# Down projection summed on VectorE in running PSUM sums, norm roots on GpSimd, and tails with a new order

## The chip, the cores and the metric

The kernel runs on one core of one Trainium2 chip. The metric is the device time of one execution, in microseconds (us). A core has TensorE (PE: matrix multiplications from SBUF into PSUM), VectorE (DVE) and ScalarE (ACT) for elementwise work, GpSimd (POOL), and SyncE (SP), which here issues the transfers between DRAM and SBUF. Each engine takes its instructions in order and waits for semaphores of the others.

## What is computed

A two-layer encoder on 1024 rows of width 1024, in float32. Each layer is a mixing half (dilated attention beside latent attention in layer 0, a gated block beside neighbourhood attention in layer 1) and a dense FFN of hidden width 2816. Every half starts with an RMSNorm.

```python
def _rmsnorm(x, g):
    y = xf * lax.rsqrt(jnp.mean(xf * xf, -1, keepdims=True) + EPS) * g
...
    for layer in range(DEPTH):
        h = _rmsnorm(x, norm_mix[layer])
        ...
            x = x + jnp.concatenate([a_out, b_out], -1) @ ev_w_out[j]
        ...
            x = x + jnp.concatenate([c_out, d_out], -1) @ od_w_out[j]
        h = _rmsnorm(x, norm_ffn[layer])
        gu = h @ ffn_w_gu[layer]
        x = x + (jax.nn.silu(gu[..., :FFN_HIDDEN]) * gu[..., FFN_HIDDEN:]) @ ffn_w_down[layer]
    return _rmsnorm(x, final_gain)
```

## The kernel before

Every float32 multiplication is made as three: an operand is split into a high part (ScalarE copies it, rounded, L61) and a low part (VectorE or GpSimd subtracts, L62), and `mm3` (L67 to L71) multiplies high by high, low by high and high by low into one PSUM tile. Large products use Winograd's scheme: both matrices are cut into quarters, seven products of sums of quarters are formed instead of eight, and sums of these give the result.

The **projections** (gate and up of the FFN, and those into a layer) are lists of `Block`s. A block makes the seven weight operands (`combo`), multiplies each with an activation operand and adds up (`post`). The activation operands are named after their sums: `B1` (a first quarter pair), `T0` to `T3` (four sums), `B2`; each has a high and a low part (`B1h`, `B1l`). Product 1 and 2 use `B1`, 5 `T0`, 6 `T1`, 7 `T2`, 4 `T3`, 3 `B2`. `FIRST` is the order of the seven in the first block.

A **tail** stands at the end of each half that feeds the next norm. `tail` goes over eight tiles of 128 rows in the order 0, 1, 4, 2, 5, 3, 6, 7. In each it multiplies the last four chunks of the contraction (24 matmuls of 128x512), adds into x (L1038), takes the norm (`norm_pre`: square with its sum on ScalarE, `rstd_from_ssq`, then `nh` on VectorE, L121), transposes the normed tile on TensorE two tiles later (`ops_tile`, L967) and makes the operands from the transposed tile: tiles 0 to 3 give `B1` and a raw copy `rw`, tiles 4 to 7 with the raw copy of the tile four before give `T0` to `T3` and `B2`. The last two tiles and the first projection products are interleaved by `first`. There are three such tails (tail 1 behind layer 0's output projection, tail 2 behind its FFN, tail 3 behind layer 1's output projection), and one that ends in the output instead of operands; its last tile is worked by halves (`last_tile`).

The **root** (`rstd_from_ssq`) is a square root on ScalarE, a reciprocal on VectorE and one Newton step in four more VectorE instructions.

The **down projection** (`down`) takes 18 of the FFN's 22 chunks of 128 in Winograd's scheme (the other four are the tail's). Seven products, each in five groups of two chunks (the last of one); an item is one product and group, two chunks by four row tiles by three, 24 matmuls. It reads hidden activations `a1`, `a2` and a streamed `st` (from the DRAM tile `hS`) and weights `b1`, `b2`, `b3`. `prep` makes the two operands and their splits, two items ahead of the matmuls; `load` issues the transfers four items ahead. The order of products is 1, 7, 5, 6, 2, 3, 4. A product's two PSUM tiles are added into the quarters of x that need it (`post`). GpSimd makes the sums of the activations (L1227, L1231, L1235, L1239) and six sums into x (L1273); VectorE makes those of the weights (L1228, L1232, L1236, L1242) and the splits.

The order on each engine is set by a scheduler from the order in which the program is written and its priorities; `high_priority` raises a part.

## Time and profile before

| | us |
|---|---|
| median of 3 runs (2534.26 to 2544.32) | 2538.3 |
| profiled execution | 2536.99 |
| its span | 2535.2 |
| TensorE busy | 2427.9 (96%) |
| VectorE busy | 1815.4 (72%) |
| ScalarE busy | 1095.0 (43%) |
| GpSimd busy | 422.5 (17%) |

The busy share is an average over stages. A stage is read from the table by stretches: its length, less the time in which TensorE is busy, is time in which TensorE stood still there. PEclk is the mean clock granted to TensorE, 1.00 being 2.4 GHz and 0.50 being 1.2 GHz. The view of waits then says which instruction waited, on which engine's instruction, and for how long.

### The profile page before, as it was taken

The numbers are of one execution on the slowest core, as the hardware profiler recorded it, in microseconds if no ns is written. First come the engines' busy times: TensorE is split into PE (matmuls) and PEld (weight loads), VectorE is DVE, ScalarE is ACT, GpSimd is POOL, SyncE is SP. The second block draws the span as 40 slices with busy tenths as digits, with TensorE's granted clock in tenths as the row PEclk, the third lists the DMA queues.
The fourth block names the chain that finished last, engine by engine and source line by source line (L and its number), as shares of the span: only waits on it lengthen the run. The fifth ranks groups of instructions, "written<-read, shape, count | busy, mean of one in ns | idle before, by whom it ended". The sixth has DMA issues, their size and how long they took to land.

```text
span 2535.2 us, 31630 instructions
## 1 busy us (share of the span) xinstructions
PE 2427.9 (96%) x12205; PEld 2047.1 (81%) x12205; DVE 1815.4 (72%) x2324; ACT 1095.0 (43%) x1691; POOL 422.5 (17%) x247
## 2 busy tenths in 40 slices
...
GB/s 259 154 195 222 270 172 142 109 141 72 116 185 92 65 99 100 50 100 222 205 54 142 120 164 162 127 180 202 197 107 100 64 87 100 62 140 271 75 63 67
DMA packets 199670, 345.76 MB, mean 136 GB/s; under 512 B 12936, under 2 KB 122728, under 8 KB 199264
## 3 DMA queue, kind: packets, MB, share of 16 engines
...
## 4 chain that ended last, share of the span: by engine, by line
PE 71%; DVE 15%; ACT 4%; issue 4%; DMA 4%; POOL 2%; SPq 0%; DVEq 0%; ACTq 0%; POOLq 0%
PE b L69 20%; PE b L70 20%; PE b L71 20%; DVE wl L62 3%; PE m L807 2%; PE b L693 2%; PE b L791 2%; DMA T2l<-rpk 1%; PE m L732 1%; PE b L711 1%; DVE bPl L62 1%; DVE T2h L62 1%; DVE xt L1038 1%; POOL rw L991 1%; DMA raw<-in_ffn_w_gu_dram 1%
## 5 line engine op out<-in xcount | busy, mean ns | idle before, releaser
L61 ACT ACTIVATE wh<-sr 128x1024 fp32r<-128x1024 f32 (+1 forms) x121 | 126.1, 1045 | 348.7 <-PE b L70 325.2
L1751 DVE TENSOR_TENSOR u<-u,b 128x1024 f32<-128x1024 f32 (+1 forms) x119 | 141.2, 1204 | 139.5 <-PE b L71 139.4
L61 ACT ACTIVATE wh<-raw 128x1024 fp32r<-128x1024 f32 (+1 forms) x102 | 105.9, 1050 | 244.2 <-PE b L70 135.3
L62 DVE TENSOR_TENSOR wl<-sr,wh 128x1024 fp32r<-128x1024 f32 (+1 forms) x121 | 146.0, 1209 | 53.1 <-ACT wh L61 52.9
L70 PE MATMUL b<-B1l,wh 128*128 128x512 f32 x440 | 171.7, 390 | 0.8 <-DVE rs_v L97 0.8
L69 PE MATMUL b<-B1h,wh 128*128 128x512 f32 x440 | 171.4, 390 | 0.0
L71 PE MATMUL b<-B1h,wl 128*128 128x512 f32 x440 | 171.3, 389 | 0.0
L1227 POOL TENSOR_TENSOR B2l<-raw,T3h 128x1024 f32<-128x1024 f32 x2 | 6.9, 3442 | 816.2 <-PE b L70 816.2
L70 PE MATMUL b<-wl,wh 128*128 128x512 f32 x336 | 132.1, 393 | 7.8 <-DVE wl L62 7.7
L71 PE MATMUL b<-wh,wl 128*128 128x512 f32 x336 | 130.9, 389 | 0.0
L69 PE MATMUL b<-wh,wh 128*128 128x512 f32 x336 | 130.8, 389 | 0.0
L69 PE MATMUL b<-wh,mh 128*128 128x512 f32 x320 | 128.7, 402 | 0.8 <-DVE B1l L1057 0.8
L62 DVE TENSOR_TENSOR wl<-raw,wh 128x1024 fp32r<-128x1024 f32 (+1 forms) x96 | 115.3, 1210 | 17.9 <-ACT wh L61 17.4
L70 PE MATMUL b<-wl,mh 128*128 128x512 f32 x320 | 127.5, 398 | 0.0
L71 PE MATMUL b<-wh,ml 128*128 128x512 f32 x320 | 127.1, 397 | 0.1
L70 PEld LDWEIGHTS b<-B1l,wh 128*128 128x128 f32 x440 | 82.6, 188 | 18.7 <-DVE B1l L973 1.7
L71 PEld LDWEIGHTS b<-B1h,wl 128*128 128x128 f32 x440 | 82.6, 188 | 17.0
L69 PEld LDWEIGHTS b<-B1h,wh 128*128 128x128 f32 x440 | 82.6, 188 | 17.0
L62 DVE TENSOR_TENSOR bPl<-b,bPh 128x1024 fp32r<-128x1024 f32 x64 | 78.0, 1220 | 13.0 <-ACT bPh L61 12.4
L70 PEld LDWEIGHTS b<-wl,wh 128*128 128x128 f32 x336 | 63.1, 188 | 25.4 <-DVE wl L62 12.6
L69 PE MATMUL b<-T1h,wh 128*128 128x512 f32 x192 | 75.6, 394 | 7.5 <-ACT wh L61 7.5
L784 DVE CUSTOM_DVE_ANT_0 bP<-b,zero 128x1024 f32<-128x1024 f32 x64 | 77.9, 1217 | 6.7 <-PE b L71 4.2
...
## 6 DMA issues: line engine op xcount, KB each, us to landing
raw<-in_ffn_w_gu_dram SPq DMA_DIRECT2D x88, 512.0 KB, 5.0
hS<-hid SPq DMA_DIRECT2D x44, 512.0 KB, 2.9
xt<-xp SPq DMA_DIRECT2D x24, 512.0 KB, 4.3
x<-xt SPq DMA_DIRECT2D x24, 512.0 KB, 2.7
raw<-in_od_w_in_dram SPq DMA_DIRECT2D x20, 512.0 KB, 6.1
raw<-kS SPq DMA_DIRECT2D x16, 512.0 KB, 6.7
st<-hS SPq DMA_DIRECT2D x16, 512.0 KB, 4.0
raw<-in_ev_w_in_dram SPq DMA_DIRECT2D x14, 512.0 KB, 5.0
```

The source lines that it names most:

```text
L61: nc.scalar.activation(hi, src, AF.Copy)
L62: (eng or nc.vector).tensor_tensor(lo, src, hi.bitcast(F32), ALU.subtract)
L69: mm(ps, lhsT=l[0], rhs=r[0], start=start, stop=False)
L70: mm(ps, lhsT=l[0], rhs=r[1], start=False, stop=False)
L71: mm(ps, lhsT=l[1], rhs=r[0], start=False, stop=stop)
L693: nc.tensor.matmul(sp[:, tt, j0:j1], lhsT=q, rhs=k[l], start=l == 0, stop=l == 1)
L711: nc.tensor.transpose(tp[:, pos], sb[:, tt, kc * P:(kc + 1) * P], self.ident)
L732: nc.tensor.matmul(o, lhsT=v, rhs=pt[l][:, pp], start=first, stop=last)
L784: nc.vector.tensor_tensor_reduce(pr, sp, self.zero.to_broadcast([P, S]), 1.0, 3e38, ALU.add, ALU.min, st[:, 0, hd, t:t + 1])
L791: nc.tensor.transpose(tp[:, kc], pr[:, kc * P:(kc + 1) * P], self.ident)
L807: nc.tensor.matmul(o, lhsT=V[:, kc], rhs=pt[l][:, kc], start=(kc == 0 and l == 0), stop=(kc == KC - 1 and l == 1))
L1751: add = lambda o, x: k.nc.vector.tensor_tensor(o, x, pb, ALU.add)
```

## The change

- **Root**: a scaling on GpSimd (VectorE where there are eight columns) and a power with exponent -0.5 on GpSimd take the place of ScalarE's root and VectorE's five steps.
- **Tail**: the last two tiles' `nh` are made on VectorE like the others (`VIAP` goes); the fourth tile's split of `B1` is made from PSUM at raised priority, ahead of the raw copy, and its transposes and those of the last two tiles no longer stand early; of the two sums into the raw copy of tiles 4 to 7 one (`x[0]`) moves from GpSimd to VectorE; the x buffer is three deep, and the operand sum of product 5 uses it. `FIRST` becomes 1, 2, 5, 4, 6, 7, 3, and the low parts of products 1 and 2 of the first block move from GpSimd to VectorE.
- **Down**: the order of products becomes 1, 5, 6, 3, 7, 2, 4. Products 1, 6, 7, 4 add up in the same PSUM tiles without a reset, and so do 5, 3. After each product its running sum is added into one quarter of x. All operand sums are on VectorE. `st` is streamed for products 5, 3, 7 and 4, and `b2` is loaded a second time into `B2h` for product 7.
- **Last tile**: each half has a PSUM tile of its own; x is multiplied by the gain before the root is known; then ScalarE scales one half and VectorE the other.

```diff
         r = self.t(pool, [P, w], F32, "rs_r")
-        nc.scalar.activation(s, ssq, AF.Sqrt, scale=1.0 / n, bias=self.eps)
-        nc.vector.tensor_scalar(v, ssq, 1.0 / n, EPS, ALU.mult, ALU.add)
-        nc.vector.reciprocal(r, s)
...
+        (nc.gpsimd if w == 1 else nc.vector).tensor_scalar(r, ssq, 1.0 / n, EPS, ALU.mult, ALU.add)
+        nc.gpsimd.tensor_tensor(r, r, self.mhalf[:, :w], ALU.pow)
         return r
...
         if t < 4:
+            with self.tc.high_priority(offset=200) if t == 3 else nullcontext():
+                self.split(o["B1"][0][:, :, sl], o["B1"][1][:, :, sl], pt)
             raw = raws[t] = self.t(wk, [P, 8, P], F32, "rw", bufs=self.rwb)
             nc.scalar.activation(raw, pt, AF.Copy)
-            nc.scalar.activation(o["B1"][0][:, :, sl], pt, AF.Copy)
-            tt_(o["B1"][1][:, :, sl], raw, o["B1"][0][:, :, sl].bitcast(F32), ALU.subtract)
             return
...
         T = [self.t(wk, [P, 4, P], F32, "tt", bufs=2) for i in range(2)]
-        tt_(T[0], pt[:, :4], raw[:, :4], ALU.subtract)
+        x = [raw[:, 4 * i:4 * i + 4] for i in range(2)]
+        tt_(T[0], pt[:, :4], x[0], ALU.subtract)
         tt_(T[1], pt[:, 4:], T[0], ALU.subtract)
-        for i in range(2):
-            x = raw[:, 4 * i:4 * i + 4]
-            nc.gpsimd.tensor_tensor(x, T[1], x, ALU.subtract)
...
+        nc.gpsimd.tensor_tensor(x[1], T[1], x[1], ALU.subtract)
+        tt_(x[0], T[1], x[0], ALU.subtract)
+        for i, y, eng in ((0, T[0], None), (3, x[1], nc.gpsimd), (1, T[1], None), (2, x[0], None), ("B2", pt[:, 4:], None)):
+            self.split(o[i][0][:, :, sl], o[i][1][:, :, sl], y, eng=eng)
...
-            elif p[0] in HPS:
-                with self.tc.high_priority(offset=HPO):
-                    self.ops_tile(wk, ps, p[1], p[0], raws)
             else:
...
             if out is None:
-                x = self.t(wk, [P, D], F32, "xt", bufs=2)
+                x = self.t(wk, [P, D], F32, "xt", bufs=3)
                 self.dma(nc.sync, x, xpart[sl])
...
                 self.split(m[0][:, ks], m[1][:, ks], msrc[:, ks, sl], eng=nc.gpsimd)
+            if out is not None and n == 7:
+                self.last_tile(wk, m, ws, [self.t(ps, [P, 2, 512], F32, "b")[:, 0] for i in range(2)], x, gain, out[sl])
+                break
             pb = self.t(ps, [P, 2, 512], F32, "b")
-            if out is not None and n == 7:
-                self.last_tile(wk, m, ws, pb, x, gain, out[sl])
-                break
             for k in range(4):
...
                 self.dma(nc.sync, xdst[sl], x)
-            hist.append((t, self.norm_pre(wk, x, gain, pb.rearrange("p c n -> p (c n)") if n in VIAP else None)))
+            hist.append((t, self.norm_pre(wk, x, gain)))
             if out is not None:
...
             for k in range(4):
-                self.mm3(pb[:, cc], (m[0][:, k], m[1][:, k]), [w[:, cs[cc]] for w in ws[k]], k == 0, k == 3)
-            nc.vector.tensor_tensor(x[:, cs[cc]], x[:, cs[cc]], pb[:, cc], ALU.add)
+                self.mm3(pb[cc], (m[0][:, k], m[1][:, k]), [w[:, cs[cc]] for w in ws[k]], k == 0, k == 3)
+            nc.vector.tensor_tensor(x[:, cs[cc]], x[:, cs[cc]], pb[cc], ALU.add)
             nc.scalar.activation(h[:, cs[cc]], x[:, cs[cc]], AF.Square, accum_out=ss[:, cc:cc + 1])
+            nc.vector.tensor_tensor(x[:, cs[cc]], x[:, cs[cc]], gain[:, cs[cc]], ALU.mult)
         ssq = self.t(wk, [P, 1], F32, "ssq", bufs=4)
...
         r = self.rstd_from_ssq(wk, ssq, D)
-        for cc in range(2):
-            nc.vector.scalar_tensor_tensor(h[:, cs[cc]], x[:, cs[cc]], r, gain[:, cs[cc]], ALU.mult, ALU.mult)
-            self.dma(nc.sync, out[:, cs[cc]], h[:, cs[cc]])
+        nc.scalar.activation(h[:, cs[0]], x[:, cs[0]], AF.Copy, scale=r)
+        nc.vector.tensor_scalar(h[:, cs[1]], x[:, cs[1]], r, None, ALU.mult)
+        for c in cs:
+            self.dma(nc.sync, out[:, c], h[:, c])
...
-        items = [(p, g) for p in (1, 7, 5, 6, 2, 3, 4) for g in range(len(groups))]
+        chain = {1: (1, 6, 7, 4), 5: (5, 3), 2: (2,)}
+        head = {p: c for c, ps_ in chain.items() for p in ps_}
+        items = [(p, g) for p in (1, 5, 6, 3, 7, 2, 4) for g in range(len(groups))]
-        dve, pool = nc.vector.tensor_tensor, nc.gpsimd.tensor_tensor
+        dve = nc.vector.tensor_tensor
...
         def load(p, g):
+            n = groups[g][1]
             if p == 1:
                 l = (("a1", hS, 0, 0), ("b1", W, 0, 0))
-            elif p == 7:
-                l = (("a2", hS, 0, 1), ("b2", W, 0, 1), ("b3", W, 1, 1))
+            elif p == 5:
+                l = (("a2", hS, 0, 1), ("b2", W, 0, 1))
+            elif p == 6:
+                l = (("b3", W, 1, 1),)
             elif p == 2:
                 l = (("a1", hS, 1, 0), ("b1", W, 1, 0))
-            elif p in (5, 4):
-                t = strm[p, g] = self.t(z, [P, 2, 512], F32, "st", bufs=2)[:, :groups[g][1]]
-                self.dma(nc.sync, t, quarter(hS, 1, 1, g))
-                l = ()
             else:
...
                 self.dma(nc.sync, tile_(name, g), quarter(src, j, c, g))
-            if p in (7, 5) and g < 4:
-                t = 4 * (p == 5) + g
+            if p in (5, 3, 7, 4):
+                t = strm[p, g] = self.t(z, [P, 2, 512], F32, "st", bufs=2)[:, :n]
+                self.dma(nc.sync, t, quarter(hS, p != 7, p != 3, g))
+            if p == 7 and g < 2:
+                load_b2(g)
+            if p in (5, 6) and g < 4:
+                t = 4 * (p == 6) + g
                 self.dma(nc.sync, x[t // 4][:, t % 4], xin[t * P:(t + 1) * P])
+        def load_b2(g):
+            t = strm["w", g] = shared("B2h")[:, g % 2 * 1024:g % 2 * 1024 + groups[g][1] * 512].rearrange("p (a n) -> p a n", n=512)
+            self.dma(nc.sync, t, quarter(W, 0, 1, g))
...
                 a, b = a1, b1
-            elif p == 7:
-                a, b = [shared("B2l")[:, y:y + n * 512].rearrange("p (a n) -> p a n", n=512) for y in (0, 1024)]
-                pool(a, a1, a2, ALU.subtract)
-                dve(b, b3, b2, ALU.subtract)
             elif p == 5:
                 a, b = a2, b2
-                pool(a2, a2, strm[p, g], ALU.add)
+                dve(a2, a2, strm[p, g], ALU.add)
                 dve(b2, b2, b1, ALU.subtract)
...
                 a, b = a2, b2
-                pool(a2, a2, a1, ALU.subtract)
+                dve(a2, a2, a1, ALU.subtract)
                 dve(b2, b3, b2, ALU.subtract)
...
                 a, b = a2, b3
-                pool(a2, a1, a2, ALU.subtract)
+                dve(a2, strm[p, g], a2, ALU.subtract)
+            elif p == 7:
+                a, b = strm[p, g], strm["w", g]
+                dve(a, a1, a, ALU.subtract)
+                dve(b, b3, b, ALU.subtract)
             else:
...
             w[p, g] = ops
+            if p == 7 and g + 2 < len(groups):
+                load_b2(g + 2)
...
             if g == 0:
-                pbs[p] = [self.t(ps, [P, 2, 512], F32, "b") for h in range(2)]
+                pbs[p] = (pbs[head[p]] if head[p] != p else
+                          [self.t(ps, [P, 2, 512], F32, "b") for h in range(2)])
             A, B = w.pop((p, g))
...
                     self.mm3(pbs[p][t // 2][:, t % 2], [v[:, a, t * P:(t + 1) * P] for v in A], [v[:, a] for v in B],
-                             k + a == 0, k + a == NK - 1)
-        s = [shared("B2h")[:, y:y + 1024].rearrange("p (a n) -> p a n", n=512) for y in (0, 1024)]
+                             k + a == 0 and head[p] == p, k + a == NK - 1, head[p] != p)
...
         def post(p):
+            i, j = {1: (0, 0), 5: (1, 1), 6: (0, 1), 3: (0, 1), 7: (1, 1), 2: (0, 0), 4: (1, 0)}[p]
             for h in range(2):
-                pb = pbs[p][h]
-                if p == 1:
-                    nc.scalar.activation(s[h], pb, AF.Copy)
-                elif p == 6:
-                    dve(s[h], s[h], pb, ALU.add)
-                    for i, j in ((0, 1), (1, 0), (1, 1)):
-                        pool(c(i, j, h), c(i, j, h), s[h], ALU.add)
-                for i, j in {1: ((0, 0),), 7: ((1, 0), (1, 1)), 5: ((1, 1), (0, 1)), 2: ((0, 0),), 3: ((0, 1),),
-                             4: ((1, 0),)}.get(p, ()):
-                    dve(c(i, j, h), c(i, j, h), pb, ALU.add)
-                if xpart is not None and p in (3, 4):
+                c = x[i][:, 2 * h:2 * h + 2, j * 512:(j + 1) * 512]
+                dve(c, c, pbs[p][h], ALU.add)
+                if xpart is not None and p in (2, 4):
                     r = 4 * (p == 4) + 2 * h
...
 LAST = (1, 2, 6, 7, 5, 4, 3)
-FIRST = (1, 2, 5, 6, 7, 4, 3)
+FIRST = (1, 2, 5, 4, 6, 7, 3)
...
         elif i == 5:
-            s[1] = k.t(k.wk, [P, 1024], F32, *(("sr", 2) if not k.ahead else ("sx", 1)))[:, :self.n]
+            s[1] = k.t(k.wk, [P, 1024], F32, *(("sr", 2) if not k.ahead else ("xt", 3)))[:, :self.n]
             tt_(v(s[1]), a(1, 0), a(1, 1), ALU.add)
...
         if src is not None:
-            k.split(v(hi), v(lo), src, eng=nc.gpsimd if self.order == FIRST and i in (1, 2) else None)
+            k.split(v(hi), v(lo), src)
         self.c[i] = (hi, lo)
...
```

The first place is VectorE in the first down projection. Before, in the operand work of product 7 (`B2l` and `b_` hold weight and activation sums, `wl` and `T2h`, `T2l` low parts):

```order
L1228 TENSOR_TENSOR B2l_9985<-b_1605_9982,b_1604_9980 128x1024
L62 TENSOR_TENSOR T2h_10069<-B2l_9985,T2h_10069 128x1024
L1232 TENSOR_TENSOR b_1604_9980<-b_1604_9980,T1h_9849 128x1024
L62 TENSOR_TENSOR T2l_10072<-B2l_9985,T2l_10072 128x1024
L62 TENSOR_TENSOR wl_10107<-B2l_9985,wh_10106 128x1024
L1228 TENSOR_TENSOR B2l_9985<-b_1613_10024,b_1612_10022 128x1024
L1232 TENSOR_TENSOR b_1612_10022<-b_1612_10022,T1l_9852 128x1024
```

After, in the operand work of product 5 (`st` is the streamed activation):

```order
L1206 TENSOR_TENSOR T3h_9775<-T3h_9775,st_9778 128x1024
L1206 TENSOR_TENSOR T0h_9813<-T0h_9813,st_9816 128x1024
L1207 TENSOR_TENSOR b_1551_9851<-b_1551_9851,T1h_9718 128x1024
L58 TENSOR_TENSOR wl_9859<-T3h_9775,wh_9858 128x1024
L58 TENSOR_TENSOR wl_9863<-T3h_9775,wh_9862 128x1024
L1206 TENSOR_TENSOR T0l_9849<-T0l_9849,st_9853 128x1024
L1207 TENSOR_TENSOR b_1558_9892<-b_1558_9892,T1l_9721 128x1024
```

Sums of weights alone stood there before (L1228, L1232); now the sums of activations with `st` (L1206) stand on VectorE too.

The second place is GpSimd at the end of tail 1. Before (`ml` is the low part of a tail operand, `rw` a raw copy, `wl` the low part of weights, `nh` x times gain):

```order
L62 TENSOR_TENSOR ml_7076<-mixB_2561,mh_7075 128x512
L991 TENSOR_TENSOR rw_6836<-tt_7029,rw_6836 128x512 x2
L985 TENSOR_TENSOR T3l_6644<-rw_6836,T3h_6643 128x4x128
L62 TENSOR_TENSOR wl_7141<-raw_7134,wh_7140 128x1024
L115 TENSOR_TENSOR nh_7058<-xt_7000,gain_6648 128x1024
L62 TENSOR_TENSOR wl_7145<-raw_7137,wh_7144 128x1024
L115 TENSOR_TENSOR nh_7119<-xt_7073,gain_6648 128x1024
```

After (`rs_r` is the root):

```order
L58 TENSOR_TENSOR ml_6954<-mixB_2489,mh_6953 128x512
L90 TENSOR_SCALAR rs_r_6882<-ssq_6880 128x1
L91 TENSOR_TENSOR rs_r_6882<-rs_r_6882,mhalf_63 128x1
L962 TENSOR_TENSOR rw_6745<-tt_6915,rw_6745 128x512
L58 TENSOR_TENSOR T3l_6572<-rw_6745,T3h_6571 128x4x128
L90 TENSOR_SCALAR rs_r_6947<-ssq_6945 128x1
L91 TENSOR_TENSOR rs_r_6947<-rs_r_6947,mhalf_63 128x1
L90 TENSOR_SCALAR rs_r_7000<-ssq_6998 128x1
L91 TENSOR_TENSOR rs_r_7000<-rs_r_7000,mhalf_63 128x1
```

The weights' low parts and the products with the gain have left GpSimd, and pairs of root steps stand between the sums.

The third place is VectorE there, from the sum of the last tile but one. Before (`rs_` are the root's steps, `sx` product 5's operand sum):

```order
L1038 TENSOR_TENSOR xt_7000<-xt_7000,b_7006 128x1024
L973 TENSOR_TENSOR B1l_6627<-rw_7101,B1h_6626 128x8x128
L97 TENSOR_SCALAR rs_v_7062<-ssq_7059 128x1
L1038 TENSOR_TENSOR xt_7073<-xt_7073,b_7079 128x1024
L98 RECIPROCAL rs_r_7064<-rs_s_7063 128x1
L100 SCALAR_TENSOR_TENSOR rs_q_7065<-rs_r_7064,rs_v_7062 128x1
L104 TENSOR_SCALAR rs_q_7065<-rs_q_7065 128x1
L105 TENSOR_TENSOR rs_r_7064<-rs_r_7064,rs_q_7065 128x1
L62 TENSOR_TENSOR wl_7149<-sx_7150,wh_7148 128x1024
```

After (`xt_7020` is product 5's operand sum):

```order
L1005 TENSOR_TENSOR xt_6886<-xt_6886,b_6892 128x1024
L58 TENSOR_TENSOR wl_7011<-raw_7004,wh_7010 128x1024
L58 TENSOR_TENSOR B1l_6555<-b_6970,B1h_6554 128x8x128
L101 SCALAR_TENSOR_TENSOR nh_6944<-xt_6886,rs_r_6947,gain_6576 128x1024
L1005 TENSOR_TENSOR xt_6951<-xt_6951,b_6957 128x1024
L58 TENSOR_TENSOR wl_7015<-raw_7007,wh_7014 128x1024
L1668 TENSOR_TENSOR xt_7020<-raw_7004,raw_7007 128x1024
L101 SCALAR_TENSOR_TENSOR nh_6997<-xt_6951,rs_r_7000,gain_6576 128x1024
L58 TENSOR_TENSOR wl_7019<-xt_7020,wh_7018 128x1024
```

The root's steps are gone; the last two `nh` and the weights' low parts stand there, and product 5's sum has moved behind the last tile's addition.

The fourth place is VectorE in the last tile. Before:

```order
L1057 TENSOR_TENSOR B1l_18364<-B1l_18364,b_19893 128x512
L1060 TENSOR_TENSOR ssq_19924<-ss_3060_19895 128x1
L97 TENSOR_SCALAR rs_v_19926<-ssq_19924 128x1
L98 RECIPROCAL rs_r_19928<-rs_s_19927 128x1
L100 SCALAR_TENSOR_TENSOR rs_q_19929<-rs_r_19928,rs_v_19926 128x1
L104 TENSOR_SCALAR rs_q_19929<-rs_q_19929 128x1
L105 TENSOR_TENSOR rs_r_19928<-rs_r_19928,rs_q_19929 128x1
L1063 SCALAR_TENSOR_TENSOR nh_19894<-B1l_18364,rs_r_19928,gain_19571 128x512 x2
```

After, from the last tile but one's `nh`:

```order
L101 SCALAR_TENSOR_TENSOR nh_19585<-B1l_18114,rs_r_19588,gain_19325 128x1024
L1024 TENSOR_TENSOR B1l_18114<-B1l_18114,b_19597 128x512
L1026 TENSOR_TENSOR B1l_18114<-B1l_18114,gain_19325 128x512
L1024 TENSOR_TENSOR B1l_18114<-B1l_18114,b_19598 128x512
L1026 TENSOR_TENSOR B1l_18114<-B1l_18114,gain_19325 128x512
L1028 TENSOR_TENSOR ssq_19631<-ss_2937_19600 128x1
L1031 TENSOR_SCALAR nh_19599<-B1l_18114,rs_r_19633 128x512
```

Each half's addition is followed by a multiplication with the gain, which stands ahead of the other half's addition.

## Rows read from the trace of the kernel before

**Rows 1.** Table by stretches: stretch, length, busy time (count) of engines, PEclk, DMA share, GB/s.
```profile
720.00:800.00 80.00, 66.89 (x309) 54.07 (x308) 67.65 (x93) 45.10 (x67) 39.03 (x21) 0.96 0.31 108
1220.00:1330.00 110.00, 99.84 (x423) 80.30 (x422) 109.48 (x68) 38.16 (x42) 71.47 (x24) 0.97 0.30 100
1420.00:1466.00 46.00, 37.38 (x237) 33.73 (x237) 40.70 (x54) 27.31 (x40) 30.43 (x15) 0.93 0.23 81
1840.00:1900.00 60.00, 49.87 (x226) 40.32 (x225) 53.28 (x70) 35.24 (x52) 35.12 (x18) 0.94 0.27 95
2320.00:2430.00 110.00, 99.33 (x423) 79.90 (x422) 109.46 (x68) 38.29 (x42) 71.43 (x24) 0.97 0.29 100
```
**Rows 2.** The three longest waits of TensorE in tail 1: total us, times, longest.
```profile
PE b L69 <- ACT wh L61: 3.8, 1, 3.8
PE b L967 <- DVE rs_v L97: 3.2, 1, 3.2
PE b L967 <- ACT nh L117: 3.0, 2, 1.5
```
**Rows 3.** Longest wait of TensorE in the first down projection; the second has its like.
```profile
PE b L70 <- DVE T2l L62: 6.5, 1, 6.5
```
**Rows 4.** Timeline of VectorE in the first down: start, length, instruction.
```profile
1235.96 3.36 DVE L62 TENSOR_TENSOR T2l<-B2l,T2l 128x1024 fp32r<-128x1024 f32 x1
```
**Rows 5.** Timeline of GpSimd in the same stretch.
```profile
1234.92 3.32 POOL L1227 TENSOR_TENSOR B2l<-T1l,a 128x1024 f32<-128x1024 f32 x1
```
**Rows 6.** Groups by shape, VectorE and ScalarE: busy us, mean ns, then idle before.
```profile
L1276 DVE TENSOR_TENSOR B1h<-B1h,b 128x1024 f32<-128x1024 f32 x16 | 18.9, 1207 | 0.0
L121 DVE SCALAR_TENSOR_TENSOR nh<-xt,rs_r,gain 128x1024 f32<-128x1024 f32 x19 | 24.4, 1282 | 0.5
L119 ACT ACTIVATE nh<-xt 128x1024 f32<-128x1024 f32 x19 | 20.1, 1058 | 29.6 <-DVE xt L1038 27.0 <-DMA xt<-in_x_dram 2.6
```
**Rows 7.** Timeline of VectorE in tail 1.
```profile
765.88 1.43 DVE L973 TENSOR_TENSOR B1l<-rw,B1h 128x1024 fp32r<-128x1024 f32 x1 [2.04 <-ACT B1h L972]
...
769.82 2.12 DVE L105 TENSOR_TENSOR rs_r<-rs_r,rs_q 128x1 f32<-128x1 f32 x1
```
**Rows 8.** Timeline of GpSimd in the same stretch.
```profile
766.19 3.39 POOL L115 TENSOR_TENSOR nh<-xt,gain 128x1024 f32<-128x1024 f32 x1
769.53 2.39 POOL L62 TENSOR_TENSOR wl<-raw,wh 128x1024 fp32r<-128x1024 f32 x1
```
**Rows 9.** Groups by shape, GpSimd: the undisturbed `nh`, and its shortest operations.
```profile
L62 POOL TENSOR_TENSOR ml<-mixB,mh 128x128 fp32r<-128x128 f32 x4 | 2.8, 712 | 0.6 <-ACT mh L61 0.6
L115 POOL TENSOR_TENSOR nh<-B1l,gain 128x1024 f32<-128x1024 f32 x1 | 2.4, 2378 | 5.0 <-DVE B1l L1038 5.0
...
L1927 POOL MEMSET const-float32-1.0<- 128x1 f32 x1 | 0.1, 99 | 0.0
```
**Rows 10.** Timeline of TensorE, its last two matmuls: their starts are 0.23 apart.
```profile
2527.37 0.39 PE L70 MATMUL b<-wl,mh 128*128 128x512 f32 x1
2527.60 0.39 PE L71 MATMUL b<-wh,ml 128*128 128x512 f32 x1
```
**Rows 11.** DMA issues: count, KB each, median us from issue to landing.
```profile
st<-hS SPq DMA_DIRECT2D x16, 512.0 KB, 4.0
```
**Rows 12.** Wait of TensorE in the first 20 us.
```profile
PE b L967 <- DVE nh L121: 1.5, 1, 1.5
```
**Rows 13.** Timeline of VectorE in the last microseconds.
```profile
2521.58 1.22 DVE L1038 TENSOR_TENSOR B1l<-B1l,b 128x1024 f32<-128x1024 f32 x1 [0.62 <-PE b L71]
...
2528.02 0.69 DVE L1057 TENSOR_TENSOR B1l<-B1l,b 128x512 f32<-128x512 f32 x1 [2.37 <-PE b L71]
...
2529.69 0.15 DVE L97 TENSOR_SCALAR rs_v<-ssq 128x1 f32<-128x1 f32 x1
...
2530.85 1.41 DVE L1063 SCALAR_TENSOR_TENSOR nh<-B1l,rs_r,gain 128x512 f32<-128x512 f32 x2
```
**Rows 14.** Timeline of ScalarE there: the square of the last half.
```profile
2528.74 0.63 ACT L1058 ACTIVATE nh<-B1l 128x512 f32<-128x512 f32 x1 [1.85 <-DVE B1l L1057]
```

48 lines of the change are left out of this document (8 added, 40 removed).

## The prediction

> **What bounds the kernel now.** I read the page first: TensorE is busy nearly all the time, VectorE three quarters, GpSimd a sixth. The change leaves TensorE its work (10,862 rows in its order before and after), so the most it can give back is time in which TensorE stands still or runs at its lower clock in the stages it touches. Then the table by stretches for the three tails and the two down projections [rows 1]. Length less PE busy is idle time; (1 - PEclk) times length is what the lower clock cost. Tail 1 (720 to 800): 80 - 66.9 = 13.1 idle and 0.04 x 80 = 3.2, so 16.3 us. Down 1: 10.2 + 3.3 = 13.5. Tail 2: 8.6 + 3.2 = 11.8. Tail 3: 10.1 + 3.6 = 13.7. Down 2: 10.7 + 3.3 = 14.0. In all 69.3 us, of which tails 41.8 and downs 27.5. Outside them the change touches the first microseconds and the last tile.
>
> Then the waits. In tail 1 TensorE waits for a root, twice for the `nh` that ScalarE scales, and for the fourth product's weights [rows 2]. In each down it has one long wait, 6.5 us in product 7 [rows 3]. The instruction streams say why: VectorE's split there takes 3.36 us [rows 4], with GpSimd's sums of 3.3 us beside it [rows 5], where a 128x1024 VectorE operation takes 1.21 undisturbed [rows 6].
>
> **Why VectorE is slow there.** In tail 1 VectorE's `rs_r` on 128x1 starts at 769.82 and takes 2.12 us [rows 7]; it ends at 771.94, and GpSimd's `wl` runs from 769.53 to 771.92 [rows 8]. So a VectorE operation with both inputs in SBUF waited out a GpSimd operation. It goes the other way too: GpSimd's `nh` starts at 766.19, VectorE's `B1l` (both inputs in SBUF) ends at 767.31, and `nh` takes 3.39 us against 2.38 for the same operation beside an idle VectorE [rows 7 to 9].
>
> **The down projections.** Removed from each: on GpSimd 20 operand sums (16 of 128x1024, four of half) and six sums into x, on ScalarE two copies, on VectorE four additions into x. Added: VectorE does the 20 sums; products 1, 6, 7, 4 add up in one pair of PSUM tiles and 5, 3 in another, so each product needs two additions; `st` is streamed for four products rather than two, and `b2` loaded a second time, 16 more issues on SyncE. TensorE needs 24 matmuls per item of two chunks at 0.23 us [rows 10], 5.44 us, and 24.5 us for a product. VectorE without GpSimd beside it: two splits and at most two sums, 4 x 1.21 = 4.84 us an item, so 4.5 x 4.84 + 2.4 = 24.2 us for each of products 5, 6 and 7, of 24.5 available, and less for the other four. It fits by a hair, and product 1 (2.4 us an item) gives a lead. Walking VectorE's new order from the start of product 1, product 5's first operands are ready at 19.9 us (needed at 24.5), 6's at 45.3 (49.0), 3's at 69.9 (73.5), 7's at about 94 (97.9); the tightest is 7's third item, 107.4 against 108.8. There the loads count: `st` and the second `b2` have two buffers each, a load lands 4.0 us after its issue [rows 11], and SyncE issues in order. VectorE's first step of product 7 stands early, ahead of the last splits of product 1, and holds these until its `b2` has landed; the walk still has them in time by several us. Wholly hidden, the downs give 27.5; I leave 1.5 in each for late loads: **24.5**. Bounds: 17 (product 7 waits 3 to 4 us with a spell of low clock in each) to 27.5.
>
> **The root on GpSimd.** Before: square root on ScalarE and five small VectorE steps, 1.16 us from the sum to the use (2529.69 to 2530.85 [rows 13]). After: a scaling and a power on 128x1, both on GpSimd. The trace has no power. Nearest below: MEMSET of one column, 0.10 us; above: a TENSOR_TENSOR of 128 columns, 0.71 [rows 9]. Two such steps with their hand-overs lie between 0.4 and 1.6; I take 1.0, nearer the upper row, because operands are read and written as there. To it comes the lock shown above: in a tail about half of VectorE's time goes to operations with both inputs in SBUF, and either GpSimd step can wait up to 1.28 us [rows 6]. I add 0.4, so **R = 1.4**; bounds 0.4 and 1.6 + 2 x 1.28 = 4.2.
>
> The Trainium skill, "SBUF — State Buffer", section "Who interferes with whom", says that a VectorE instruction with two SBUF inputs and a GpSimd instruction that reads SBUF contend, and that whichever issues first blocks the other for its whole length. The trace agrees (2.12 us for one column). It speaks for the downs and against a root on GpSimd: were both steps of every root to meet a full VectorE operation, R would be 3.6 and the sum below only 8 us.
>
> **The tails.** The transposes of the fourth tile and of the last two now stand in the middle of a tile or of product 1, as those of the others do. A tile's chain to them (addition 1.2, square 1.06 + 0.2, R, `nh` 1.28 [rows 6]) takes 3.8 + R, and some 9 us pass on TensorE; but VectorE, in order, has the sums and splits of the earlier tiles ahead of it. The ScalarE-scaled `nh` (two waits of 1.5) goes. Product 4 now stands ahead of 6, whose late `sr` weights (wait 3.8) get 5.4 us more. Walking PE, ScalarE, VectorE and GpSimd through tail 1 with R = 1.2 leaves three waits: product 1, 4.5 us, because the fourth tile's B1 split stands on ScalarE behind five splits of the tile before it, which hang in a chain through VectorE and GpSimd, and two weight splits; the last transposes, 1.1; product 5 on the last tile's `T0l`, 2.8. With 1.8 for low clock after them 10.2 remain. Tail 3 has the same order, so 10.2 too; in tail 2 B1's late part is needed later, and 3.3 + 0.7 + 1.1 with 1.2 of clock, 6.3, remain. Gain 41.8 - 26.7 = 15.1. A us more of R costs some 3.5 in a tail (the fifth transposes have 0.1 us of slack, and product 1 and the last two tiles follow), 10.5 in three; the 0.2 by which R exceeds 1.2 takes 2.1: **13.0**. Bounds: 28 at R = 0.4 with the waits at product 1 halved; -16 at R = 4.2. The weight splits of the first two products, moved from GpSimd to VectorE, are in the walk.
>
> **Head and end.** At the start the 1.5 us wait for the second `nh` [rows 12] shrinks as five VectorE steps go: **1.0** (0 to 2). The three roots of eight columns swap short steps for short steps: 0. At the end the half additions no longer share a PSUM tile with their matmuls, but the gain multiplication of a half waits for ScalarE's square of it and stands ahead of the next step on VectorE. From the end of the seventh tile's matmuls, E = 2521.6: addition 1.2, square 1.26 and root 1.2 to 3.7; `nh` to 5.0; addition 0.69, square 0.8, multiplication 0.69 and the same for the second half to 9.4; the sum, root 1.2 and scaling 0.63 to 11.3. Before, the last `nh` ends at 2532.26, E + 10.7 [rows 13, 14]. **Loss 0.6**; each us of R counts twice.
>
> **Sum.** 24.5 + 13.0 + 1.0 - 0.6 = 37.9. The profiled run took 2537.0 us (span 2535.2), 1.3 under the median of the three, so 2537.0 - 37.9 = 2499.
>
> **Rivals.**
> (a) VectorE becomes the bound in the downs: 24.2 us of work per 24.5 in three products. If its steps take 5% more, 1 us is lost in each of 5, 6 and 7, and as much again by loads: 6 per down, 12 in all, 2511. For: the margin. Against: 1.21 is the mean of busy stretches.
> (b) The lock makes R 2.6, 1.2 more; a us of R costs 10.5 in tails, 2 at the end and 1 at the start, 13.5: 2499 + 16 = 2515. For: rows 7 and 8. Against: half of VectorE's time in a tail goes to operations with one input in PSUM.
> (c) The power itself is slow, several us a call, and stands in GpSimd's queue ahead of the next sums. The gain is used up at R = 1.4 + 37.9 / 13.5 = 4.2; slower by 0.5% from 5.1; at R = 6, 2499 + 62 = 2561. For: nothing in the trace times a power. Against: it has one element per partition.
> (d) GpSimd's first power costs some 6 us once, ahead of the first `nh`: 2505. Against: GpSimd's steps in the trace start right behind their input. The Trainium skill, "GPSIMD Engine Reference", section "Instruction dispatch", tells of a code load of about 6 us at the first call of a freshly loaded kernel; no run here shows one.
> (e) The walks are too cautious: tails keep 13 us rather than 29 and the downs nothing: 2499 - 16 - 3 = 2480.
>
> **How the numbers follow.** Chances: forecast 0.50, (a) 0.13, (b) 0.13, (c) 0.05, (d) 0.05, (e) 0.14. Range 2478 to 2518: it leaves out (c) and the far ends of the others. 0.5% (12.7 us) is about what a measurement can tell here, so faster means below 2525.6. Slower is (c) past R = 5.1, 0.04; the same is (c) below that and (a) with (b) together, 0.08; faster 0.88.
>
> **What would show it.** Right: no 6.5 us wait in either down, VectorE's 128x1024 steps all near 1.2 there, PEclk 1.0; in the tails a wait of about 4 us at product 1 for B1, none for an `nh` from ScalarE; the two root steps together 1.0 to 1.6. Wrong: waits of several us in product 7 for `st` or `B2h`; roots over 2 us; the middle transposes of every tile late by the same amount.

## The result, and the profile after

The changed kernel takes 2494.8 us (median of 4 runs, 2489.7 to 2499.2) against 2541.0 for the kernel before in the same session: ratio 0.983, 95% interval 0.981 to 0.985. The forecast was 2499 (2478 to 2518). The profiled execution took 2493.2, its span 2491.3, 43.9 us shorter than before. The total came close; two of its terms did not, and one step is wrong in a way that the total hides.

The table by stretches of the changed kernel, for the same five stages in the same order (tail 1, down 1, tail 2, tail 3, down 2) as [rows 1]. Columns: stretch, length, busy time and count of PE, PEld, DVE, ACT and POOL, then PEclk, DMA share, GB/s.

```profile
713.00:793.00 80.00, 75.02 (x347) 61.33 (x346) 61.14 (x60) 40.90 (x60) 28.59 (x30) 0.96 0.38 133
1200.00:1320.00 120.00, 120.00 (x531) 99.42 (x530) 101.18 (x97) 44.43 (x49) 0.00 (x0) 1.00 0.57 195
1370.00:1420.00 50.00, 46.65 (x230) 39.13 (x229) 35.25 (x35) 26.87 (x40) 19.87 (x24) 0.95 0.44 158
1795.00:1865.00 70.00, 64.75 (x303) 52.77 (x302) 54.44 (x55) 36.41 (x54) 28.56 (x30) 0.95 0.30 110
2275.00:2395.00 120.00, 120.00 (x531) 99.43 (x530) 101.51 (x98) 44.34 (x49) 0.00 (x0) 1.00 0.57 194
```

Read as in the prediction (length less PE busy, plus (1 - PEclk) times length): the two downs lose nothing now, where they lost 27.5. Tail 1 loses 5.0 + 3.2 = 8.2, tail 2 3.4 + 2.5 = 5.9, tail 3 5.3 + 3.5 = 8.8: 22.8 in all where it was 41.8, so the tails gave back 19.0. GpSimd's busy time is 0.00 in both downs.

TensorE's waits in tail 1 (715 to 805; total us, times, longest), in place of [rows 2]:

```profile
PE b L66 <- ACT B1h L57: 2.6, 1, 2.6
PE b L67 <- DVE B1l L58: 1.7, 1, 1.7
PE b L66 <- ACT T0h L57: 0.4, 1, 0.4
PE b L67 <- DVE T0l L58: 0.2, 1, 0.2
```

No `nh` is waited for any more. In tail 2 the largest wait is 2.6 us, for a `wl` of VectorE. In tail 1 product 1 waits 2.6 + 1.7 = 4.3 us for the fourth tile's `B1`; TensorE's clock falls to its lower level behind that wait (two stretches of 4 us from 764 show what the engine did and what clock it had):

```profile
764.00:768.00 4.00, 1.23 (x3) 0.83 (x4) 4.00 (x4) 2.82 (x5) 0.74 (x2) 0.80 0.33 131
768.00:772.00 4.00, 4.00 (x11) 3.09 (x10) 3.80 (x4) 1.58 (x4) 1.12 (x2) 0.50 0.33 131
```

The root itself: the groups of its two lines over the whole program (durations in ns, least, median, most), then GpSimd's and VectorE's timeline in tail 1 (start, length, instruction, idle time before it).

```profile
L90 POOL TENSOR_SCALAR rs_r<-ssq x40: 190/190/1056, 5.5 to 2486.2; 128x1 f32<-128x1 f32 x40
L91 POOL TENSOR_TENSOR rs_r<-rs_r,mhalf x43: 546/550/1670, 5.8 to 2486.5; 128x1 f32<-128x1 f32 x40, 128x8 f32<-128x8 f32 x3
```
```profile
766.21 0.19 POOL L90 TENSOR_SCALAR rs_r<-ssq 128x1 f32<-128x1 f32 x1 [2.95 <-ACT nh L99]
766.48 0.55 POOL L91 TENSOR_TENSOR rs_r<-rs_r,mhalf 128x1 f32<-128x1 f32 x1
770.80 1.05 POOL L90 TENSOR_SCALAR rs_r<-ssq 128x1 f32<-128x1 f32 x1 [3.77 <-ACT nh L99]
...
770.59 1.21 DVE L1668 TENSOR_TENSOR xt<-raw,raw 128x1024 f32<-128x1024 f32 x1
```

A root takes 0.19 + 0.55 us and a gap, 766.21 to 767.03 = 0.82. The second one here met VectorE's sum of two SBUF operands, which ends at 771.80: GpSimd's small step ends with it, at 771.85, and took 1.05 us. That is the lock of [rows 7, 8], but the median of 40 steps is 190 ns: only the last tile's root of each tail met it for 1.05 us (so that this root takes 1.7), and one near 24 us for 0.5.

**What the change did elsewhere.** In the first 20 us the wait for the second `nh` is 0.6 us, where it was 1.5 [rows 12]; but TensorE has two new waits near 90 us, where before it had one of 0.3:

```profile
PE b L947 <- DVE nh L101: 0.6, 1, 0.6
...
PE b L66 <- ACT wh L57: 1.6, 1, 1.6
PE b L68 <- DVE bPl L58: 0.8, 1, 0.8
```

`ops_tile` serves layer 0's first projections too, and its list of splits now has the one that those weights wait for (`bPl`) last; before it came first. And the 8-column root for the queries: GpSimd's timeline, then VectorE's, then the stretch from 240 to 256 of the kernel before and of the changed one.

```profile
247.01 1.65 POOL L91 TENSOR_TENSOR rs_r<-rs_r,mhalf 128x8 f32<-128x8 f32 x1 [1.39 <-DVE rs_r L90]
...
248.70 1.66 DVE L506 TENSOR_SCALAR sacc<-ident,rs_r 128x128 f32<-128x128 f32 x8 [1.77 <-POOL rs_r L91]
```
```profile
240.00:256.00 16.00, 12.61 (x54) 9.19 (x54) 7.86 (x20) 4.85 (x8) 6.37 (x3) 1.00 0.77 278
...
240.00:256.00 16.00, 12.90 (x46) 8.51 (x46) 7.25 (x15) 5.60 (x8) 4.16 (x3) 0.79 0.72 265
```

Idle time there is 3.4 and 3.1 us, but 0.21 x 16 = 3.4 us more go to the lower clock. TensorE's own waits around this root (225 to 270) did not grow: 3.7 us in all before, 3.1 now.

The end: E, the end of the last tile but one's matmuls, is 2477.2 now.

```profile
2486.20 0.19 POOL L90 TENSOR_SCALAR rs_r<-ssq 128x1 f32<-128x1 f32 x1 [5.71 <-DVE ssq L1028]
2487.05 0.72 ACT L1030 ACTIVATE nh<-B1l,rs_r 128x512 f32<-128x512 f32 x1 [1.81 <-POOL rs_r L91]
2487.57 0.81 SPq L52 DMA_DIRECT2D out_dram<-nh  x2
```

The last `nh` ends at 2487.77, E + 10.6 (before E + 10.7), and the span ends 14.1 after E, before 13.6. From the last `nh` to the end of the span it is now 3.5 us, before 2.9. The halves are now ready together, so that both transfers are issued in one piece from 2487.57, one right behind the other; that this is where the 0.6 us go is likely, but no run shows it.

### The profile page after: what moved, and what is told of

Read it like the earlier page. It is cut to its first block, busy times and chain, and to the rows that moved or that the text cites. A ratio compares the mean times of both kernels' runs of the same rounds, so it can differ in the third digit from the quotient of the medians.

```text
span 2491.3 us, 31387 instructions
## 1 busy us (share of the span) xinstructions
PE 2416.3 (97%) x12205; PEld 2044.4 (82%) x12205; DVE 1740.5 (70%) x2171; ACT 1062.4 (43%) x1630; POOL 235.0 (9%) x249
## 4 chain that ended last, share of the span: by engine, by line
PE 81%; DVE 10%; ACT 3%; issue 2%; DMA 2%; POOL 1%; SPq 0%; POOLq 0%; DVEq 0%; ACTq 0%
PE b L66 24%; PE b L67 23%; PE b L68 23%; PE m L787 2%; PE b L673 2%; PE b L771 2%; PE m L712 1%; DVE nh L101 1%; PE b L691 1%; DVE wl L58 1%; DVE bPl L58 1%; DMA T2l<-rpk 1%; DVE rw L963 1%; DVE xt L1005 1%; DVE bP L764 1%
## 5 line engine op out<-in xcount | busy, mean ns | idle before, releaser
L58 POOL TENSOR_TENSOR ml<-msrc,mh 128x512 fp32r<-128x512 f32 x16 | 21.7, 1361 | 1183.9 <-ACT mh L57 1183.9
L66 PEld LDWEIGHTS b<-B1h,wh 128*128 128x128 f32 x440 | 83.5, 190 | 25.3 <-ACT B1h L57 6.0
L766 ACT ACTIVATE bP<-bP,stB 128x1024 f32<-128x1024 f32 x64 | 73.3, 1146 | 16.2 <-DVE stB L764 15.8
L1721 DVE TENSOR_TENSOR cc<-u,b 128x1024 f32<-128x1024 f32 (+1 forms) x36 | 42.8, 1190 | 48.1 <-PE b L68 48.1
```

The lines of the kernel that those rows point to most:

```text
L58: (eng or nc.vector).tensor_tensor(lo, src, hi.bitcast(F32), ALU.subtract)
L66: mm(ps, lhsT=l[0], rhs=r[0], start=start, stop=False, skip_group_check=more)
L766: nc.scalar.activation(pr, pr, AF.Exp, scale=-1.0, bias=st[:, 0, hd, t:t + 1], accum_out=st[:, 1, hd, t:t + 1])
L1721: add = lambda o, x: k.nc.vector.tensor_tensor(o, x, pb, ALU.add)
```

## Experiments

Each is measured against the kernel before on the same chip; "changed" is the changed kernel (ratio 0.983). The runs stand on several chips, so where two numbers are given for a difference one is worked out from the ratios and one from the medians.

### e1_down_only

The kernel before with the new `down` and `mm3` alone; tails, roots and last tile stay.

> The kernel before with the new down projection alone (its sums on VectorE, running sums in PSUM, its order of products); tails, root and last tile as before. Theory: the downs account for 28 us of the change, apart from the tails: 28 us under the kernel before, and TensorE without a wait over 0.5 us in either down. Rival (the stages help one another, by a shared queue or buffer): clearly less than 24, or more than 33.

2508.5 us (2507.7 to 2512.1), ratio 0.989 (0.987 to 0.991): 28 to 30 us less, so the rival falls. The first down's stretch:

```profile
1208.00:1328.00 120.00, 120.00 (x531) 99.38 (x530) 102.17 (x98) 45.20 (x48) 0.00 (x0) 1.00 0.54 183
```

TensorE never stands still in it, nor in the second down (2290 to 2440), so the whole 27.5 of [rows 1] came, and no load was late for it.

### e2_gpsimd_sums

The changed kernel with the 20 sums of activations of each down back on GpSimd; the running sums in PSUM stay.

```diff
-        dve = nc.vector.tensor_tensor
+        dve, pool = nc.vector.tensor_tensor, nc.gpsimd.tensor_tensor
...
-                dve(a2, a2, strm[p, g], ALU.add)
+                pool(a2, a2, strm[p, g], ALU.add)
...
-                dve(a2, a2, a1, ALU.subtract)
+                pool(a2, a2, a1, ALU.subtract)
...
-                dve(a2, strm[p, g], a2, ALU.subtract)
+                pool(a2, strm[p, g], a2, ALU.subtract)
...
-                dve(a, a1, a, ALU.subtract)
+                pool(a, a1, a, ALU.subtract)
```

> The changed kernel with one thing put back: the 20 sums of activations in each down on GpSimd; order of products, running sums in PSUM and additions into x stay new. Theory (operations of VectorE and GpSimd that both read two SBUF tiles wait for one another): VectorE's 128x1024 steps beside those sums take about 3.3 us again, waits of TensorE come back, 15 to 30 us over the changed kernel. Rival (the gain came from the running sums, the order of products and the fewer additions into x): within 4 us of the changed kernel.

2523.5 us (2520.6 to 2525.2), ratio 0.995 (0.993 to 0.996), 29 to 30 us over changed: all of the downs' gain is gone again. VectorE and GpSimd in down 1, and TensorE's waits there (1200 to 1340):

```profile
1218.12 3.30 DVE L1211 TENSOR_TENSOR T3h<-T3l,T3h 128x1024 f32<-128x1024 f32 x1
1221.34 3.40 DVE L1207 TENSOR_TENSOR b<-b,T1l 128x1024 f32<-128x1024 f32 x1
...
1216.96 3.37 POOL L1210 TENSOR_TENSOR T3h<-T3h,raw 128x1024 f32<-128x1024 f32 x1
1220.30 3.37 POOL L1206 TENSOR_TENSOR a<-a,st 128x1024 f32<-128x1024 f32 x1
```
```profile
PE b L67 <- DVE wl L58: 8.6, 3, 4.4
PE b L67 <- DVE T2l L58: 1.9, 2, 1.7
```

The same VectorE sums that take 1.22 us in the changed kernel take 3.3 to 3.4 beside GpSimd: they take turns. VectorE's first one here ends at 1221.42, 1.1 us behind the end of GpSimd's first (1220.33), which is about the time that it takes alone. So the gain comes from clearing GpSimd of these sums; with them on GpSimd, running sums, the order of products and fewer additions are worth nothing. Whether the sums on VectorE would give it without the running sums, no run tries. The Trainium skill, "SBUF — State Buffer", section "Who interferes with whom", says that one of the two blocks the other for a whole instruction; these rows agree.

### e7_old_down

The changed kernel with the `down` of before.

> The changed kernel with the old down projection: tails, root and last tile new alone. Theory (the parts add up): 14 to 17 us under the kernel before, the downs with their 6.5 us wait as before. Rival (the tails need the new down, say for free buffers or queues): under 8.

2524.8 us (2521.8 to 2526.8), ratio 0.995 (0.993 to 0.997): 12.7 to 14 us less than before, under the 14 to 17 expected. With e1's 28 to 30 that makes 41 to 44, and the whole change gave 43.7 by its ratio: the two halves of the change add up. Its tail 1 is as in the changed kernel:

```profile
713.00:793.00 80.00, 75.12 (x347) 61.22 (x346) 61.05 (x61) 41.18 (x60) 28.60 (x30) 0.96 0.38 132
```

Tails 2 and 3 lose 4.9 and 8.9 us here (1385 to 1435, 1812 to 1882), so the tails give their 19 in this kernel too, and some 6 are lost elsewhere: the 2.1 at 90 us, the 3.1 near the queries' root and the 0.5 at the end shown above, less 0.9 in the first 20 us, and some 2 in the neighbourhood attention (30.1 lost in 1620 to 1820, before 27.7 in 1630 to 1830), which the change does not touch.

### e3b_old_root

The changed kernel with the root of before (ScalarE's square root, five VectorE steps) everywhere; order of the tails and last tile stay. (A first form, e3_old_root, also kept the constant that the power needs; its tail buffers needed 44.25 kB per partition where 44.22 were left, so there is no time of it.)

```diff
-        (nc.gpsimd if w == 1 else nc.vector).tensor_scalar(r, ssq, 1.0 / n, EPS, ALU.mult, ALU.add)
-        nc.gpsimd.tensor_tensor(r, r, self.mhalf[:, :w], ALU.pow)
+        nc.scalar.activation(s, ssq, AF.Sqrt, scale=1.0 / n, bias=self.eps)
+        nc.vector.tensor_scalar(v, ssq, 1.0 / n, EPS, ALU.mult, ALU.add)
+        nc.vector.reciprocal(r, s)
...
```

> The changed kernel with the root of before (a square root on ScalarE, then five small steps on VectorE); the order of the tails, the raised priority, the last tile's halves and the new down stay. Theory: in the changed kernel the end of a tail hangs on the root of the last two tiles, which there takes 0.82 us from sum of squares to root (0.19 and 0.55 us on GpSimd). The root of before takes 1.4 us where nothing disturbs it and four places in VectorE's queue, which in a tail is the engine that is waited for; by 3.5 us per us of root in each of three tails that is 6 us, and with the small steps on VectorE 6 to 10: 2501 to 2505 us against 2494.8. Rival (the gain of the tails comes from the order and the raised priority, and the root's place is of no matter): within 3 us of the changed kernel.

2509.2 us (2502.1 to 2512.9), ratio 0.988 (0.986 to 0.990): 13 to 14 over changed, above the 6 to 10 of the theory, and the rival (within 3) falls. Its three tails, and TensorE's longest wait in the first:

```profile
720.00:800.00 80.00, 70.83 (x327) 58.06 (x326) 65.95 (x99) 42.54 (x68) 22.03 (x14) 0.94 0.37 125
1380.00:1450.00 70.00, 61.07 (x339) 53.10 (x339) 60.26 (x94) 39.89 (x63) 21.47 (x14) 0.95 0.34 121
1820.00:1890.00 70.00, 60.82 (x284) 49.79 (x283) 63.58 (x91) 39.35 (x60) 19.38 (x12) 0.95 0.27 98
```
```profile
PE b L958 <- DVE nh L112: 6.7, 3, 5.3
```

They lose 14.0 + 12.4 + 12.7 = 39.1 us, 16.3 more than in the changed kernel. Of the tails' 19.0, then, 16 hang on the root's new place and under 3 are had by the rest without it; no run separates the parts of that rest, the raised priority among them. The total is no measure of the tails alone: in the first 20 us of this kernel TensorE also waits 5.8 us for the second `nh`, which stands behind three splits on VectorE, where it waits 0.6 in the changed kernel and 1.5 in the kernel before [rows 12].

### e4_slow_root

The changed kernel with each one-column root made longer.

```diff
+        for i in range(4 if w == 1 else 0):
+            nc.gpsimd.tensor_scalar(r, r, 1.0, 0.0, ALU.mult, ALU.add)
```

> The changed kernel with four more small steps (times 1, plus 0) on GpSimd behind each one-column root: by 0.19 us a step and the gaps between such steps 0.8 to 1.1 us more from sum of squares to root. Nothing else moves. Theory: three tails end with a root on the path, at 3.5 us of TensorE's time per us of root in each, and the end of the kernel with one more: 3 x 3.5 x 0.8 to 1.1 plus 1 gives 9.5 to 12.5 us over the changed kernel, 2504 to 2507. Rival (the root has slack after the change, and the tails end with the weights' splits and product 1): under 4 us.

2521.3 us (2515.5 to 2523.7), ratio 0.993 (0.991 to 0.994): 25 to 26.5 over changed, more than twice the price of the theory. The three tails, a root of tail 1, and then VectorE's waits in tail 1 (735 to 785), of this kernel and, below the dots, of the changed one:

```profile
725.00:805.00 80.00, 68.61 (x302) 54.44 (x301) 60.15 (x59) 38.48 (x57) 31.62 (x55) 0.91 0.26 93
1390.00:1470.00 80.00, 70.57 (x443) 63.20 (x442) 62.64 (x61) 37.58 (x54) 28.83 (x48) 0.96 0.32 112
1825.00:1905.00 80.00, 68.82 (x295) 54.55 (x294) 63.29 (x62) 37.25 (x53) 26.86 (x46) 0.91 0.23 80
```
```profile
753.78 0.19 POOL L90 TENSOR_SCALAR rs_r<-ssq 128x1 f32<-128x1 f32 x1 [1.28 <-ACT nh L101]
754.05 0.55 POOL L91 TENSOR_TENSOR rs_r<-rs_r,mhalf 128x1 f32<-128x1 f32 x1
754.69 1.01 POOL L93 TENSOR_SCALAR rs_r<-rs_r 128x1 f32<-128x1 f32 x4
```
```profile
DVE nh L103 <- POOL rs_r L93: 15.4, 5, 3.9
...
DVE nh L101 <- POOL rs_r L91: 7.2, 4, 2.2
```

The root now takes 1.9 us, 1.1 more. The tails lose 49.6 us: 32.0 of idle time (13.6 in the changed kernel) and 17.6 by the clock (9.2), 26.8 more together; the two profiled spans differ by 26.0, so nearly all of it lies in the tails. The idle part alone is 18.4 / 3 / 1.1 = 5.6 us per us of root in a tail: VectorE waits out a root five times in this stretch, since `nh` stands right behind the addition in its queue, and its later sums and splits stand behind `nh`. The lower clock adds 2.5 to that. The four steps also stand ahead of GpSimd's own sums, and how much of the price is theirs, the run does not tell.

### e11_short_root

The changed kernel with a root of the power alone.

```diff
-        (nc.gpsimd if w == 1 else nc.vector).tensor_scalar(r, ssq, 1.0 / n, EPS, ALU.mult, ALU.add)
-        nc.gpsimd.tensor_tensor(r, r, self.mhalf[:, :w], ALU.pow)
+        if w > 1:
+            nc.vector.tensor_scalar(r, ssq, 1.0 / n, EPS, ALU.mult, ALU.add)
+        nc.gpsimd.tensor_tensor(r, r if w > 1 else ssq, self.mhalf[:, :w], ALU.pow)
...
-        nc.scalar.activation(h, xt, AF.Square, accum_out=ssq)
+        nc.scalar.activation(h, xt, AF.Square, scale=1.0 / 32, accum_out=ssq)
```

> The changed kernel with a one-column root of one GpSimd step in place of two: the square on ScalarE takes the mean's scale with it, and the small added constant is left out, so that only the power remains. The root gets 0.27 us shorter (0.19 us and the gap of 0.08 behind it), from 0.82 to 0.55 us. Theory (the walk's price holds on this side: 3.5 us per us of root in each of three tails, 2 at the end, 1 at the start): 13.5 x 0.27 = 3.6 us under the changed kernel, 2490. Second theory (the price that e4_slow_root showed, 24 us per us of root, holds on both sides, since VectorE waits out every root): 6.5 us, 2487. Rival (at 0.82 us the root is no longer on the path, and product 1's operand is): under 1 us.

2485.7 us (2484.5 to 2489.2), ratio 0.979 (0.978 to 0.981): 8 to 9 under changed, nearest to the second theory's 6.5 and well over the rival's 1. The tails do not bear that out, though. TensorE's waits in tail 1:

```profile
PE b L66 <- ACT B1h L57: 4.0, 1, 4.0
PE b L948 <- DVE nh L102: 1.5, 1, 1.5
```

The tails lose 8.7 + 4.1 + 8.7 = 21.5 us by their stretches, only 1.3 less than in the changed kernel, as product 1's wait takes up what the root gives: there the rival's mechanism holds. The profiled span is 4.1 less, and its run is the slowest of the five; where the other half of the 8 us is, the one profile does not show.

### e8_tile_order

The changed kernel with another order of tiles.

```diff
-        order = range(8) if out is not None else (0, 1, 4, 2, 5, 3, 6, 7)
+        order = range(8) if out is not None else (0, 1, 4, 2, 3, 5, 6, 7)
```

(and the same list in layer 0's first projections; `rw` three deep, `xt` two.)

> The changed kernel with the tails' tiles in the order 0, 1, 4, 2, 3, 5, 6, 7 in place of 0, 1, 4, 2, 5, 3, 6, 7 (three raw copies and two input tiles in place of two and three, so that it fits). The fourth tile's product-1 operand is then ready one tile earlier. Theory (VectorE is the bound from the fifth tile to the last operand of product 5): the wait of 2.6 + 1.7 us at product 1 goes, but most of it comes back at product 5, so each tail gains 1 to 2 us: 2489 to 2493 us. Rival (product 1's wait is a cost of its own, and with it goes the half clock behind it): 4.3 us and 1.5 us of clock in tails 1 and 3, some 12 us: 2483.

2503.5 us (2496.7 to 2505.1), ratio 0.986 (0.984 to 0.987): 7 to 9 slower than changed, which neither theory had. TensorE's waits in tail 1 (715 to 805), then the largest from 70 to 100 us:

```profile
PE b L947 <- DVE nh L101: 4.5, 1, 4.5
PE b L68 <- DVE wl L58: 2.3, 1, 2.3
...
PE b L68 <- DVE bPl L58: 3.2, 2, 2.3
```

`B1` is no longer waited for in tail 1, and the wait comes back at the last tile's `nh` and the weights, larger (7.4 us of waits in place of 4.9): that a wait comes back on VectorE the theory had, but not its place and size. The lists can be told apart by stages: from 60 to 110 us layer 0 loses 8.2 us, 3.3 of them by the clock, where the changed kernel loses 2.5, so 5.7 of the 11.2 us by which the profiled span is longer are layer 0's own, and the tails (720 to 800, 1385 to 1435, 1802 to 1880) lose 27.5, 4.7 more.

### e9_three_mends, e5_wide_root, e6_split_first

The first has three edits, the others one each: 8-column roots back on ScalarE and VectorE (e5), the split of `bPl` issued first in layer 0 (e6), the last tile's second half sent first (in e9 only).

```diff
-        for i, y, eng in ((0, T[0], None), (3, x[1], nc.gpsimd), (1, T[1], None), (2, x[0], None), ("B2", pt[:, 4:], None)):
+        parts = [(0, T[0], None), (3, x[1], nc.gpsimd), (1, T[1], None), (2, x[0], None), ("B2", pt[:, 4:], None)]
+        for i, y, eng in parts[-1:] + parts[:-1] if extra else parts:
```

> The changed kernel with three places mended where its trace shows a loss against before: the 8-column roots go back to ScalarE and VectorE (GpSimd's power takes 1.65 us there and TensorE then stands at half clock), in the first projections the split that layer 0's weights wait for is issued first again, and the second half of the last tile, which is ready first, leaves first. Theory: 2.1 us at the root of the queries, 2.4 us at 90 us, 0.2 us at the end: 4.7 us under the changed kernel, 2490. Rival (those waits hide others just behind them): within 1.5 us of the changed kernel.

2484.6 us (2483.9 to 2493.2), ratio 0.980 (0.978 to 0.981): 8 to 10 under changed, about twice what was expected, and the rival (within 1.5) falls. The next three ask why.

> The changed kernel with only the three 8-column roots put back on ScalarE and VectorE, as before. e9_three_mends, which has this and two more mends, came out 10 us under the changed kernel where 4.7 was expected; this run and e6_split_first ask which mend carries it. Theory (each mend gives what its own wait cost, and the rest of the 10 us is the neighbourhood attention, whose waits differ from run to run, 36 to 45 us in the traces so far, without a change of its own): 2 to 3 us under the changed kernel, read at the root of the queries near 247 us. Rival (one mend moves later transfers and carries most of it): 5 us or more.

> The changed kernel with only the order of the splits in layer 0's first projections put back (the split that the weights wait for is issued first). Theory: 2 us under the changed kernel, all of it in the two waits of TensorE at 90 us (1.6 and 0.85 us). Rival as for the wide root: 5 us or more, found in a later stage.

> The changed kernel itself once more, beside the two, as their measure: 2494.8 us, and in its trace the same waits at 90 us and 247 us; the neighbourhood attention's waits tell how far they differ from run to run (theory: by 3 us or more; rival: by under 1 us, and then e9's 5 us there are of the mends).

The changed kernel again: 2493.8 us (2489.7 to 2497.3), ratio 0.983 (0.981 to 0.984). The wide root: 2489.6, 0.981 (0.980 to 0.982), 4 us less; its interval overlaps that of the changed kernel. The split first: 2485.0, 0.980 (0.978 to 0.981), 8 to 9 us less and as fast as all three mends, so the rival holds: one edit is enough for it. Its wait near 90 us is down to

```profile
PE b L68 <- DVE bPl L58: 0.3, 1, 0.3
```

which is 2.1 us, and not 9. The neighbourhood attention in the changed kernel, the same again, the split first and the three mends:

```profile
1604.00:1804.00 200.00, 177.19 (x1032) 148.10 (x1031) 141.54 (x308) 111.88 (x257) 57.04 (x58) 0.97 0.79 198
...
1604.00:1804.00 200.00, 177.73 (x1024) 148.04 (x1024) 140.60 (x307) 111.19 (x255) 57.07 (x58) 0.96 0.79 195
...
1598.00:1796.00 198.00, 178.67 (x1030) 148.74 (x1029) 137.07 (x307) 111.65 (x256) 57.03 (x58) 0.97 0.81 197
...
1599.00:1795.00 196.00, 182.05 (x1047) 151.71 (x1046) 137.48 (x307) 112.47 (x258) 57.63 (x58) 0.96 0.78 200
```

It loses 28.8 and 30.3 us in two profiles of one kernel, 25.3 with the split first and 21.8 with all mends. Two profiles of one kernel differ by 1.5, less than the 3 of the theory and more than the 1 of its rival, so a part of the 5.0 looks like the edit's.

Most of the 8.8 us between the profiled spans of the changed kernel (2491.9, the second time) and the split first (2483.1) is TensorE's clock. The mean granted clock is 0.987 and 0.990, and what it lacks to 1 times the span is 32 and 25 us. One place, the same work in the changed kernel and with the split first:

```profile
322.00:342.00 20.00, 17.61 (x102) 15.31 (x101) 15.58 (x26) 13.97 (x26) 0.15 (x1) 0.91 1.02 229
...
320.00:340.00 20.00, 17.76 (x117) 15.87 (x118) 17.10 (x28) 16.01 (x27) 0.30 (x2) 1.00 1.06 226
```

TensorE's waits there are the same in both (1.3 us for `aPl`, 1.1 for `stB`), and the clock falls in one alone, which costs 0.09 x 20 = 1.8 us. The like is seen near 610 us (0.91 and 1.00). Why the clock falls in one and not in the other, and how an earlier split at 90 us shortens a stage at 1600, is not settled. The intervals of the split first and of the three mends lie at the lower end of the changed kernel's or under it.

## Why the prediction came out right, and where it did not

**Downs: 24.5 forecast, 27.5 measured by the stretches and 28 to 30 by e1.** The mechanism is shown from both sides (e1, e2). The mis-sized term is the 3 us set aside for late loads: no wait for `st` or `B2h` reached TensorE, and PEclk is 1.00. VectorE is busy 101 of 120 us, so the rival that it becomes the bound (a) fell too; the tight 24.2 of 24.5 held only for three of seven products, with a lead ahead of them. (The new loads are 15 a down, ten for `st` and five for `b2`, not 16.)

**Tails: 13.0 forecast, 19.0 measured.** The failed step is the sum R = 1.4: the two steps were put at 1.0 between rows of 0.10 and 0.71 us, with 0.4 for the lock. They take 0.82, and the lock was met for a whole microsecond by one root in each tail. The walk's total for R = 1.2, 26.7 us, less 0.38 x 10.5 = 4.0 for the shorter root, gives 22.7, and 22.8 remain; but that this fits so well is luck. It had 21.9 us of idle time and 4.8 by the clock (1.8, 1.8 and 1.2), where 13.6 and 9.2 were measured, and the price of 10.5 is itself wrong, as the next paragraph shows. Of tail 1's three waits product 1's was right in place and size, 4.3 for 4.5; the last transposes' was 0 for 1.1, product 5's 0.6 (`T0h`, `T0l`) for 2.8.

**The price of a us of root: 3.5 a tail forecast; 8.1 measured for a longer root** (26.8 / 3 / 1.1, e4) **and 1.6 for a shorter one** (1.3 / 3 / 0.27, e11). This step is wrong and the total hides it. The forecast priced the fifth transposes, product 1 and the last two tiles; in e4 VectorE waits out five roots in the stretch, and the lower clock adds nearly half as much again. A root of 1.4 would, on the line between e4 and the changed kernel, have left the tails 19.0 - 0.53 x 26.8 = 4.8 us of gain, not 13.0: too long a root and too low a price cancelled for the most part: luck again. Rival (b), a root of 2.6 us at 2515, was priced too low in the same way; e4, at 1.9 us, took 2521, and 0.7 us more at 24 us a us, 17, would have used up nearly the whole gain, if the line holds so far.

**Head, +1.0 forecast.** The wait for the second `nh` shrank by 0.9, from 1.5 to 0.6, as forecast; but the two waits at 90 us, put at nothing, took 2.1, so that a loss remains. The order of the splits in `ops_tile` was read for the tails only, though layer 0 calls the same function.

**The 8-column roots, 0 forecast, a loss of about 3 in the stretch of the queries' root.** "Short steps for short steps" had no row for a power on eight columns; it takes 1.65 us, three times that of one column. Yet TensorE's waits there are no longer than before, and the loss is all lower clock. e5, with the old wide root and 2.2 us of waits there, came out 4 us lower, but its clock in the same stretch (240 to 256) is 0.79 too; e9, with the old root as well, has 1.00. So the fall of the clock does not hang on the power alone, and what brings it about stays open.

**End, -0.6 forecast, -0.5 measured,** by another way: the chain was 0.7 shorter than forecast, and 0.6 us more behind the last `nh` took it back. The forecast had used a root of 1.2 there and not its R of 1.4; with 0.82 for two roots its 11.3 becomes 10.5, and 10.6 were measured.

**The sum.** 27.5 + 19.0 + 0.9 - 2.1 - 3.1 - 0.5 = 41.7 of the 43.9 us between the profiled spans. The clock of a stretch has two digits only, and 0.005 of some 400 us of stretches is 2 us, so the other 2.2 can't be placed.

**First power (rival d).** It took 0.56 us, as the others do:

```profile
5.81 0.56 POOL L91 TENSOR_TENSOR rs_r<-rs_r,mhalf 128x1 f32<-128x1 f32 x1
```

Rival (c), a power of several us, fell with it. The Trainium skill, "GPSIMD Engine Reference", section "Instruction dispatch", has a load of about 6 us at a first call; none shows around this row, though GpSimd waited 5.1 us for ScalarE ahead of the step before it, and what lies hidden there can't be told. Rival (e), 2480, was half true: the downs had nothing to lose, and the tails lost 23 us where it had 13.
